# Moving one projection of a hybrid attention layer from direct products to seven-product units

## The chip, the cores and the metric

The kernel runs on one core of a Trainium2 chip. The metric is the device time of one execution in microseconds (us). Of the kernel before, three runs took 2165.18, 2166.86 and 2168.04 us; the median is 2166.86. A profile is one further execution, recorded instruction by instruction. Engines are named as the profile names them: PE is TensorE's matmul, PEld its weight load, DVE is VectorE, ACT is ScalarE, POOL is GpSimd and SP is SyncE, which only issues DMAs here. L631 is line 631 of the kernel.

## What is computed

The input x is 512 tokens by 2048 features, in float32. One layer is computed:

```
h = rmsnorm(x);  proj = h @ w_in          # 2048 x 6176
aq, ak, av (1024 columns each)            # 16 attention heads of 64
gq, gk (512 each), gv, gr (1024 each)     # 4 linear heads, key 128, value 256
glr (32)                                  # low-rank input of the forget gates
attn = softmax attention over three dilated windows, with a position bias
o    = gated linear attention, forward + backward, per-head rmsnorm, * silu(gr)
x    = x + concat(attn, o) @ w_out
x    = x + (silu(h2 @ w_gate) * (h2 @ w_up)) @ w_down,   h2 = rmsnorm(x)
out  = rmsnorm(x)
```

Queries of the linear heads are scaled by 128 to the power -1/2. All matrix products keep nearly float32 precision: each operand is split into a rounded part (hi, type fp32r) and its rest (lo), and three products are added: hi\*hi, hi\*lo, lo\*hi.

## The kernel before, in words

**Two ways to a product.** A *direct job* (`job`, `run_job`, L297 to L367) makes 512 output columns for all 512 tokens. It walks over 16 K-tiles of 128; a K-tile is called a half here, since two come in one weight piece of 512 KB. For each half it runs four *quarters*: one PSUM bank each, three matmuls of 128x128 by 128x512 (L337 to L339 in jobs of kind A, with weights stationary; L346 to L348 in kind B). The *seven-product* way (`Feed` from L1447, `Front` from L1659) is a fast scheme for 2x2 blocks: it makes 256 columns for 512 tokens from seven block products in place of eight. It needs sums of weight blocks (`sums`, L1423 to L1425 on VectorE), splits of them (L1436 on ScalarE, L1441 on VectorE) and sums of x's blocks (made once, in `xi`). A unit has four pieces of 14 products; each product is one matmul of 512 columns (L1532) and one of 256 (L1518). The end of a unit (`evac7`, from L1548) combines the seven banks on ScalarE and VectorE and adds parts by accumulating DMAs from GpSimd; `finish` multiplies by the rms factor of the tokens (`rb[1]`) and stores the result to a DRAM buffer.

**Order of the work.** Everything is emitted by one Python program in a fixed order, and every engine executes its own instructions in that order. The stages around the change are:

1. Two direct jobs for av, with the preparation of x (0 to 104 us).
2. `Front.run`: 12 seven-product units, four for gr and eight for aq and ak (104 to 339 us).
3. Four direct jobs: gq and gk of linear heads 0 and 1; gv of these; gq and gk of heads 2 and 3; gv of these (339 to 613 us). Their results are multiplied by the rms factor and stored (`evac_gqk`, L831 to L843: four VectorE operations and four DMAs; `evac_gv`: four ScalarE operations).
4. w_out on the attention half of its input: three jobs of eight halves and one of sixteen, whose second eight halves take the linear heads' outputs (613 to 742 us). Then the rest of w_out, and the feed-forward part with its own seven-product units.

**Side steps.** Attention and linear attention have no jobs. They are generators in a queue (`side`), and the jobs of stages 3 and 4 call them step by step between their quarters. Each quarter adds rate/4 to a credit; each whole credit is one call of `run_side(1)` (L350 to L353). The last quarter of a job adds none. The rate is `RATES[0]` = 2.5 in stage 3 and `RATES[1]` = 4.0 in stage 4. The queue holds the low-rank gate input (7 steps, made to last 14 calls by `slow`), then `attention` (from L713), then `silus` and the four linear heads (`gla`, two at a time by `turns`). A second queue, `urgent`, gets one step at each call as well.

**Attention's own order.** Attention has 64 units u (16 heads by 4 blocks of 128 queries) and makes two calls per unit. The first call of u emits the scores of u on TensorE (`att_scores`, L631 and L632), the scaling of u-2 for odd units (`att_scale`, L658, ScalarE), the exponential of u-1 (`att_exp`, L649, ScalarE) and the rounding of u-3 (`att_round`, L671, ScalarE), and every second time a copy (`att_lift`, L697). The second call emits the transposes of u-2 (`att_transpose`, L663), every second time the product with the values (`att_av`, L687 and L688), the rest of u-3 (`att_rest`, L677, VectorE), the bias and row maximum of u (`att_max`, L641, VectorE), every second time the mixing of two results (`att_mix`, L706, VectorE), then the reciprocal of u-1 (`att_norm`, L652) and, for even units, its scaling (L654). For each pair of heads, `load_qk` (L588, L592) splits queries and keys. A pair of heads' result becomes an operand of w_out, `mixh`: two heads of 64 features make one K-tile of 128, eight in all.

**Buffers.** SBUF slots come from two free lists (`s2`, 36 of 2 KB per partition, and `s4`, 33 of 4 KB), PSUM banks from a third of eight; the slot freed longest ago is taken first. A job holds four banks, and the side steps share the other four. The hi and lo parts of x (`hT`, 16 slots of `s4`) are given back by `free_h` when the first w_out job starts. Weights pass through `Stream` (from L180): a load from SP, then for each half a cast on ScalarE (L237) and a subtraction on VectorE (L218), some halves ahead of their use.

Of the kernel before, what the change touches and what calls it, by code (L numbers as in the profile page):

```python
# [112 lines left out]
def put(*slots):  # L113
    for s in slots:
        if s.home is not None:
            s.home.free.append(s.i)


def layer(nc, tc, x, attn_norm_w, w_in, rel_table, gw_f, gb_f, gw_b, gb_b, gla_norm_w, w_out,
# [7 lines left out]
    with tc.manual_schedule(), \  # L127
# [169 lines left out]
        def job(kind, pieces, kts, acts, evac, rate=0.0, before=None, start=None, limit=None):  # L297

            j = Job()
            j.kind, j.kts, j.acts, j.evac, j.rate, j.before, j.start, j.limit = \  # L300
                kind, kts, acts, evac, rate, before, start, limit
            j.first = len(st.halves)
            st.add(pieces)
            j.n = len(st.halves) - j.first
            jobs.append(j)
            return j
# [518 lines left out]
                G["gw"][d] = stacked(G["gw"][d], (0, 1), 2)  # L825
                yield

        gqd = dr.tile([8, P, 512], F32, name="gqd")
        gvd = dr.tile([4, P, 1024], F32, name="gvd")

        def evac_gqk(pr):  # L831
            def f(banks):
                for i in range(4):
                    t = s2.get()
                    if i < 2:
                        dve.scalar_tensor_tensor(t.t, banks[i].t, P ** -0.5, rb[1].t,
                                                 op0=OP.mult, op1=OP.mult)
                    else:
                        dve.tensor_tensor(t.t, banks[i].t, rb[1].t, op=OP.mult)
                    put(banks[i])  # L840
                    pool.dma_start(out=gqd[4 * pr + i], in_=t.t)
                    put(t)
            return f  # L843

        def load_gla(h):
            if h in gq:
                return
            for d, i in ((gq, 0), (gk, 2)):
                d[h] = s2.get()
                pool.dma_start(out=d[h].t, in_=gqd[h // 2 * 4 + i + h % 2])  # L850

        def load_gv(pr):
            gv[pr] = [s4.get(F32, [P, 2, 512]) for _ in range(2)]
# [371 lines left out]
                fr.late()  # L1225

        n_front = len(jobs)
        RATES = (2.5, 4.0)
        APART = 12
        for pr in range(2):  # L1230
            seg = [(w_in, C_GQ + pr * 256), (w_in, C_GK + pr * 256)]
            job("A", [piece512(seg, None, k) for k in range(0, KT, 2)], list(range(KT)), acts_h,
                evac_gqk(pr), rate=RATES[0], start=gstart if pr == 0 else None,
                before=None if pr else before_first, limit=3)
            job("B", [piece512(w_in, C_GV + pr * 512, k) for k in range(0, KT, 2)], list(range(KT)), acts_h,
                evac_gv(pr), rate=RATES[0],
                before=(lambda i: load_gates() if i == 12 else None) if pr else None)

        x1 = {}
        xd = dr.tile([16, P, 512], F32, name="xd")  # L1240
        gd = dr.tile([FF // 256, P, 1024], F32, name="gd")

        def free_h():
            for k in range(KT):
                put(*hT.pop(k))
            put(rb.pop(1))

        def load_res(c):
            x1[c] = []
# [97 lines left out]
        def start_out(c):  # L1347
            def f():
                if c == 1:
                    free_h()  # L1350
                if c != 1:
                    load_res(c)
            return f
# [17 lines left out]
        jobs[n_front + 3].lead = lambda i: AHEAD + (i > 11) + (i > 13)  # L1371
# [4 lines left out]
        for j in jobs[n_front + 4:]:  # L1376
# [282 lines left out]
        class Front(Feed):  # L1659


            def __init__(self):
                self.units = [(w_in, C_GR + g * 256) for g in range(4)] + \
                    [(w_in, c + g * 256) for g in range(4) for c in (C_AQ, C_AK)]
                self.per = NP // 2
                self.xs, self.wide, self.pre = xi, 0, {}
                self.begin([(u, q) for u in range(len(self.units)) for q in range(self.per)], 2, P)
# [520 lines left out]
```

## Time and profile before

| | |
|---|---|
| median of three runs | 2166.86 us (2165.18 to 2168.04) |
| the profiled execution | 2165.94 us, its span 2164.2 us |
| busy: PE, PEld, DVE, ACT, POOL | 2151.6, 1898.4, 1820.8, 1220.8, 355.0 us |
| granted TensorE clock | 0.999 |
| the chain that ended last, by engine | PE 96%, DVE 2%, DMA 1%, issue 1% |
| front, 104.4 to 339.4 us: PE, DVE, ACT busy | 234.48, 214.80, 123.27 of 235.00 us |
| attention beside direct jobs, 363.5 to 589.7 us | 225.35, 172.95, 160.08 of 226.20 us |
| w_out with linear attention, 613 to 742 us | 128.17, 102.83, 77.42 of 129.00 us |

The profile gives for each engine the time in which it executed something. Matmuls are pipelined: one of 512 columns shows a duration of about 0.39 us, while the next starts 0.23 us after it, so durations cannot be added; the distance between starts can. The page also follows the chain of work that ended last back from the end. A row of the waits names the waiting engine and line, the engine and line that ended the wait, the total, the number of waits and the longest. A row of the timeline gives start, duration, engine, line, operation with its operands (output, arrow, inputs), and in brackets the idle time of the engine before it and what ended that. The stage borders are read from the first and last instructions of the lines named above.

### The profile page before, as it was taken

To read this page: it belongs to the slowest core of one execution; us is meant where nothing else is said; L and a number is where in the kernel's file an instruction comes from. 1 tells how busy PE (TensorE), PEld (TensorE's weight loads), DVE (VectorE), ACT (ScalarE), POOL (GpSimd) and SP (SyncE) were. 2 spreads that over 40 slices of the span, in tenths; PEclk is the share of its full clock that TensorE was granted. 3 is DMA by queue.
4 is the path that set the end of the run, shared out by engine and by line. 5 is a ranking of instruction groups with operands and counts; after the bars stand their busy time and mean duration, and the time that the engine had idled before them with its cause. 6 is when DMAs were issued, how large, how long until landed. Compare 5 with 4: busy or idle time off the path is not lost.

```text
span 2164.2 us, 34918 instructions
## 1 busy us (share of the span) xinstructions
PE 2151.6 (99%) x12682; PEld 1898.4 (88%) x12682; DVE 1820.8 (84%) x3153; ACT 1220.8 (56%) x2228; POOL 355.0 (16%) x495
## 2 busy tenths in 40 slices
PE   9999999999999999999999999999999999999998
PEld 7888887888888889888888888888888899999987
DVE  6689996777768778899899899998989888888885
ACT  8455554777666446455555555555555655555562
POOL 0011213111011110012122112221122120021300
PEclk9999999999999999999999999999999999999999
DMA  6477779546475873567777667777776985576982
GB/s 203 138 178 182 178 179 256 153 129 184 128 259 175 268 243 112 145 179 182 184 178 192 174 180 188 177 186 181 180 196 172 266 211 176 177 180 159 283 307 79
DMA packets 264699, 405.71 MB, mean 187 GB/s; under 512 B 19341, under 2 KB 163389, under 8 KB 264526
## 3 DMA queue, kind: packets, MB, share of 16 engines
q1 hardware_dynamic: 206366, 274.59, 39.7%
q0 software_dynamic: 57840, 128.35, 26.5%
q8 instruction: 100, 1.64, 0.3%
q14 instruction: 73, 0.60, 0.1%
q10 hardware_dynamic: 320, 0.53, 0.1%
HBM read 287.47 MB, written 66.39 MB: 164 GB/s over the span
## 4 chain that ended last, share of the span: by engine, by line
PE 96%; DVE 2%; DMA 1%; issue 1%; ACT 0%; POOL 0%; DVEq 0%; ACTq 0%
PE ps L1532 31%; PE ps L1518 16%; PE ps L346 7%; PE ps L348 7%; PE ps L347 7%; PE ps L1891 5%; PE ps L1890 5%; PE ps L1889 5%; PE ps L339 1%; PE ps L337 1%; PE ps L338 1%; PE ps L663 1%; DMA b<-a 1%; PE ps L631 1%; PE ps L688 1%; PE ps L687 1%
## 5 line engine op out<-in xcount | busy, mean ns | idle before, releaser
L1436 ACT CAST b<-b 128x768 fp32r<-128x768 f32 (+1 forms) x569 | 519.0, 944 | 375.0 <-DVE b L1441 183.9
L1441 DVE TENSOR_TENSOR b<-b,b 128x768 fp32r<-128x768 f32 (+1 forms) x569 | 597.3, 1084 | 32.0 <-ACT b L1436 20.9
L1532 PE MATMUL ps<-b,b 128*128 128x512 f32 x1656 | 484.1, 393 | 0.4 <-ACT b L1436 0.2
L1532 PE MATMUL ps<-a,b 128*128 128x512 f32 x1368 | 401.1, 394 | 0.5 <-DVE b L1552 0.4
L1532 PEld LDWEIGHTS ps<-b,b 128*128 128x128 f32 x1656 | 280.8, 188 | 32.0 <-ACT b L1436 0.7
L1518 PEld LDWEIGHTS ps<-b,b 128*128 128x128 f32 x1656 | 271.4, 190 | 39.2
L1518 PE MATMUL ps<-b,b 128*128 128x256 f32 x1656 | 296.7, 280 | 0.0
L1518 PEld LDWEIGHTS ps<-a,b 128*128 128x128 f32 x1368 | 227.3, 189 | 36.9 <-DVE b L1441 0.6
L1532 PEld LDWEIGHTS ps<-a,b 128*128 128x128 f32 x1368 | 228.1, 189 | 23.1 <-issue 1.0
L1518 PE MATMUL ps<-a,b 128*128 128x256 f32 x1368 | 245.6, 280 | 0.2 <-DVE b L1441 0.2
L1423 DVE TENSOR_TENSOR b<-b 128x512 f32<-128x512 f32 x260 | 178.1, 685 | 16.5 <-DMA b<-in_w_down_dram 6.5
L1889 PE MATMUL ps<-b,b 128*128 128x256 f32 x624 | 176.6, 283 | 0.0
L1890 PE MATMUL ps<-b,b 128*128 128x256 f32 x624 | 176.6, 283 | 0.0
L1891 PE MATMUL ps<-b,b 128*128 128x256 f32 x624 | 176.6, 283 | 0.0
L346 PE MATMUL ps<-b,b 128*128 128x512 f32 x304 | 122.5, 403 | 0.0
L1889 PEld LDWEIGHTS ps<-b,b 128*128 128x128 f32 x624 | 119.8, 192 | 0.0
L1890 PEld LDWEIGHTS ps<-b,b 128*128 128x128 f32 x624 | 119.8, 192 | 0.0
L1891 PEld LDWEIGHTS ps<-b,b 128*128 128x128 f32 x624 | 119.8, 192 | 0.0
L348 PE MATMUL ps<-b,b 128*128 128x512 f32 x304 | 118.8, 391 | 0.0
L347 PE MATMUL ps<-b,b 128*128 128x512 f32 x304 | 118.6, 390 | 0.0
L1425 DVE TENSOR_TENSOR b<-b,b 128x256 f32<-128x256 f32 x260 | 110.6, 425 | 8.9
L1424 DVE TENSOR_TENSOR b<-b,b 128x256 f32<-128x256 f32 x260 | 110.5, 425 | 9.0
(303 smaller groups left out, 4176.9 us busy)
## 6 DMA issues: line engine op xcount, KB each, us to landing
b<-in_w_gate_dram SPq DMA_DIRECT2D x109, 512.0 KB, 3.9
b<-in_w_up_dram SPq DMA_DIRECT2D x88, 512.0 KB, 4.1
b<-in_w_down_dram SPq DMA_DIRECT2D x88, 512.0 KB, 5.5
b<-a POOLq DMA_DIRECT2D x162, 256.0 KB, 4.4
b<-in_w_in_dram SPq DMA_DIRECT2D x78, 512.0 KB, 3.8
b<-in_w_out_dram SPq DMA_DIRECT2D x32, 512.0 KB, 5.7
gd<-b POOLq DMA_DIRECT2D x22, 512.0 KB, 4.0
b<-gd SPq DMA_DIRECT2D x22, 512.0 KB, 7.8
```

Source lines behind the costliest of these rows:

```text
L346: mm(o, xh.t[:, c], wh.t[:, w], start=first and not on, stop=False, skip_group_check=on)
L347: mm(o, xh.t[:, c], wl.t[:, w], start=False, stop=False, skip_group_check=on)
L348: mm(o, xl.t[:, c], wh.t[:, w], start=False, stop=last, skip_group_check=on)
L1423: dve.tensor_tensor(s_[:, :, 0:2], r[:, :, 1:3], r[:, :, 0:1].to_broadcast(shape), op=OP.add)
L1425: dve.tensor_tensor(s_[:, :, 3], s_[:, :, 2], r[:, :, 3], op=OP.add)
L1436: act.copy(o, src)
L1441: dve.tensor_tensor(o, src, h, op=OP.subtract)
L1518: mm(o, wl, xh, start=False, stop=end, skip_group_check=True)
L1532: mm(o.rearrange("p (s t) -> p s t", s=2), wh, x_, start=first and p == 0, stop=False, skip_group_check=True)
L1889: mm(o, xh[:, t], wh, start=first and h == 0, stop=False, skip_group_check=True)
L1890: mm(o, xh[:, t], wl, start=False, stop=False, skip_group_check=True)
L1891: mm(o, xl[:, t], wh, start=False, stop=last, skip_group_check=True)
```

## The change

The projection gq, gk of linear heads 0 and 1 leaves the direct jobs. `Front` gets two more units, gq's first 256 columns and gk's first 256, after the four of gr; they are stored in a new buffer `gfd`, and `load_gla` reads heads 0 and 1 from it. In it, as in the other units' results, one of the two heads has its sign turned, for query and key alike, which cancels in the products. `finish` scales the query unit. One direct job of kind A is left (heads 2 and 3), then the two gv jobs. The rate of side steps in these jobs goes from 2.5 to 3.1, and attention's last steps now fall in the first w_out job. x's operands `hT` are given back K-tile by K-tile in the last direct job; `free_h` is gone.

```
-        gqd = dr.tile([8, P, 512], F32, name="gqd")
+        gqd = dr.tile([4, P, 512], F32, name="gqd")
+        gfd = dr.tile([2, P, 1024], F32, name="gfd")
...
         def load_gla(h):
             if h in gq:
                 return
-            for d, i in ((gq, 0), (gk, 2)):
+            for i, d in enumerate((gq, gk)):
                 d[h] = s2.get()
-                pool.dma_start(out=d[h].t, in_=gqd[h // 2 * 4 + i + h % 2])
+                pool.dma_start(out=d[h].t, in_=gfd[i][:, (1 - h) * 512:(2 - h) * 512] if h < 2 else gqd[2 * i + h % 2])
...
-        RATES = (2.5, 4.0)
+        RATES = (3.1, 4.0)
         APART = 12
+        seg = [(w_in, C_GQ + 256), (w_in, C_GK + 256)]
+        job("A", [piece512(seg, None, k) for k in range(0, KT, 2)], list(range(KT)), acts_h,
+            evac_gqk, rate=RATES[0], start=gstart, before=before_first, limit=3)
         for pr in range(2):
-            seg = [(w_in, C_GQ + pr * 256), (w_in, C_GK + pr * 256)]
-            job("A", [piece512(seg, None, k) for k in range(0, KT, 2)], list(range(KT)), acts_h,
-                evac_gqk(pr), rate=RATES[0], start=gstart if pr == 0 else None,
-                before=None if pr else before_first, limit=3)
-            job("B", [piece512(w_in, C_GV + pr * 512, k) for k in range(0, KT, 2)], list(range(KT)), acts_h,
-                evac_gv(pr), rate=RATES[0],
-                before=(lambda i: load_gates() if i == 12 else None) if pr else None)
+            j = job("B", [piece512(w_in, C_GV + pr * 512, k) for k in range(0, KT, 2)], list(range(KT)), acts_h,
+                    evac_gv(pr), rate=RATES[0],
+                    before=(lambda i: load_gates() if i == 12 else None) if pr else None)
+        j.drop = lambda k: put(*hT.pop(k))
...
-        def free_h():
-            for k in range(KT):
-                put(*hT.pop(k))
-            put(rb.pop(1))
...
                 if c == 1:
-                    free_h()
+                    put(rb.pop(1))
...
-                self.units = [(w_in, C_GR + g * 256) for g in range(4)] + \
+                self.units = [(w_in, C_GR + g * 256) for g in range(4)] + [(w_in, C_GQ), (w_in, C_GK)] + \
                     [(w_in, c + g * 256) for g in range(4) for c in (C_AQ, C_AK)]
...
-                    dve.tensor_tensor(c_.t, c_.t, rb[1].t[:, None, :].to_broadcast([P, 2, 512]), op=OP.mult)
-                    pool.dma_start(out=grd[u] if u < 4 else qkd[u - 4], in_=c)
+                    r = rb[1].t[:, None, :].to_broadcast([P, 2, 512])
+                    if u == 4:
+                        dve.scalar_tensor_tensor(c_.t, c_.t, P ** -0.5, r, op0=OP.mult, op1=OP.mult)
+                    else:
+                        dve.tensor_tensor(c_.t, c_.t, r, op=OP.mult)
+                    pool.dma_start(out=grd[u] if u < 4 else gfd[u - 4] if u < 6 else qkd[u - 6], in_=c)
```

`evac_gqk` is otherwise as before, without its parameter, and the indices by which later jobs are picked out of the list (`n_front + 3` and `n_front + 4`) are one lower.

More of the change, by code (lines that the diff above doesn't have):

```diff
@@ L826, in low_rank, with evac_gqk @@
                 yield
-        gqd = dr.tile([8, P, 512], F32, name="gqd")
+        gqd = dr.tile([4, P, 512], F32, name="gqd")
+        gfd = dr.tile([2, P, 1024], F32, name="gfd")
         gvd = dr.tile([4, P, 1024], F32, name="gvd")
[L831 to L843, printed above, removed]
+        def evac_gqk(banks):
+            for i in range(4):
+                t = s2.get()
+                if i < 2:
+                    dve.scalar_tensor_tensor(t.t, banks[i].t, P ** -0.5, rb[1].t,
+                                             op0=OP.mult, op1=OP.mult)
+                else:
+                    dve.tensor_tensor(t.t, banks[i].t, rb[1].t, op=OP.mult)
+                put(banks[i])
+                pool.dma_start(out=gqd[i], in_=t.t)
+                put(t)
         def load_gla(h):
@@ L1370, in layer @@
         n_in = len(jobs)
-        jobs[n_front + 3].lead = lambda i: AHEAD + (i > 11) + (i > 13)
+        jobs[n_front + 2].lead = lambda i: AHEAD + (i > 11) + (i > 13)
         j = job_out(0, 0, KT, evac_out(0), rate=RATES[1], start=start_out(0), before=load_first)
@@ L1375, in layer @@
         j.drop = lambda k: drop_mix(k) if k < 8 else None
-        for j in jobs[n_front + 4:]:
+        for j in jobs[n_front + 3:]:
             j.lead = lambda i: AHEAD + 4
@@ L1674, in do @@
                 def do():
-                    dve.tensor_tensor(c_.t, c_.t, rb[1].t[:, None, :].to_broadcast([P, 2, 512]), op=OP.mult)
-                    pool.dma_start(out=grd[u] if u < 4 else qkd[u - 4], in_=c)
+                    r = rb[1].t[:, None, :].to_broadcast([P, 2, 512])
+                    if u == 4:
+                        dve.scalar_tensor_tensor(c_.t, c_.t, P ** -0.5, r, op0=OP.mult, op1=OP.mult)
+                    else:
+                        dve.tensor_tensor(c_.t, c_.t, r, op=OP.mult)
+                    pool.dma_start(out=grd[u] if u < 4 else gfd[u - 4] if u < 6 else qkd[u - 6], in_=c)
                     put(c_)
```

## The prediction

> **What bounds the kernel now.** I read the page's engine rows first, then busy time by stage, then the waits of the attention stage, then the timeline inside it. In the stage table the columns are window, length, and busy time (instructions) of matmul, weight load, VectorE, ScalarE, GpSimd, then granted clock, DMA share and GB/s.
>
> ```profile
> PE 2151.6 (99%) x12682; PEld 1898.4 (88%) x12682; DVE 1820.8 (84%) x3153; ACT 1220.8 (56%) x2228; POOL 355.0 (16%) x495
> ```
>
> ```profile
> 104.40:339.40 235.00, 234.48 (x1345) 205.46 (x1344) 214.80 (x342) 123.27 (x203) 49.28 (x64) 1.00 0.74 184
> 363.50:589.70 226.20, 225.35 (x1220) 190.40 (x1220) 172.95 (x405) 160.08 (x337) 38.02 (x71) 1.00 0.50 150
> ...
> 613.00:742.00 129.00, 128.17 (x626) 107.38 (x626) 102.83 (x208) 77.42 (x181) 24.54 (x46) 1.00 0.68 229
> ```
>
> TensorE is busy nearly everywhere: the seven-product units of the front (104 to 339), attention beside the direct jobs (363 to 590), linear attention beside w_out (613 to 742). In the attention stage VectorE is busy 76% and ScalarE 71%, so by shares both have room. The waits of that stage (who waited for whom, total us, times, longest) say something else.
>
> ```profile
> DVE b L677 <- ACT b L671: 41.5, 44, 2.5
> ACT a L658 <- DVE small L652: 29.3, 24, 2.4
> ...
> ACT a L649 <- DVE small L641: 23.3, 28, 1.4
> ...
> DVE a L641 <- PE ps L632: 3.7, 5, 1.5
> ...
> PE ps L631 <- DVE b L677: 0.7, 1, 0.7
> ```
>
> VectorE and ScalarE wait for each other (94 us in these three rows) and hardly for TensorE (3.7). I followed that in the timeline, VectorE first, then ScalarE (start, duration, engine, line; the bracket is idle time before and who ended it).
>
> ```profile
> 508.45 0.69 DVE L677 TENSOR_TENSOR b<-ps,b 128x512 fp32r<-128x512 f32 x1 [0.75 <-ACT b L671]
> 509.06 0.68 DVE L641 CUSTOM_DVE_ANT_0 a<-ps,b 128x512 f32<-128x512 f32 x1
> ...
> 509.67 0.41 DVE L706 TENSOR_TENSOR a<-ps,a 64x256 f32<-64x256 f32 x1
> 510.00 0.14 DVE L652 RECIPROCAL small<-small 128x1 f32<-128x1 f32 x1
> 510.07 0.67 DVE L218 TENSOR_TENSOR a<-b,a 128x512 fp32r<-128x512 f32 x1
> 512.32 0.69 DVE L677 TENSOR_TENSOR b<-ps,b 128x512 fp32r<-128x512 f32 x1 [1.57 <-ACT b L671]
> 512.92 0.68 DVE L641 CUSTOM_DVE_ANT_0 a<-ps,b 128x512 f32<-128x512 f32 x1
> ...
> 514.97 0.69 DVE L677 TENSOR_TENSOR b<-ps,b 128x512 fp32r<-128x512 f32 x1 [0.16 <-ACT b L671]
> ```
>
> ```profile
> 508.72 0.62 ACT L237 CAST a<-b 128x512 fp32r<-128x512 f32 x1
> 510.24 0.72 ACT L658 ACTIVATE a<-a,small 128x512 f32<-128x512 f32 x1 [0.91 <-DVE small L652]
> 510.88 0.71 ACT L649 ACTIVATE a<-a,small 128x512 f32<-128x512 f32 x1
> ...
> 511.70 0.58 ACT L671 CAST b<-ps 128x512 fp32r<-128x512 f32 x1
> ...
> 513.65 0.73 ACT L649 ACTIVATE a<-a,small 128x512 f32<-128x512 f32 x1 [0.85 <-DVE small L641]
> ...
> 514.37 0.57 ACT L671 CAST b<-ps 128x512 fp32r<-128x512 f32 x1
> ```
>
> This is a closed loop. Call u one of the 64 units of attention (a head's block of 128 queries). The row maximum of u (L641) releases the exponential of u (L649); behind it on ScalarE stands the rounding of an older unit (L671), which releases its rest on VectorE (L677); behind that stands the maximum of u+1. That leg is 512.32 to 514.97, 2.65 us. Every second leg also holds L706, the reciprocal and the scaling on ScalarE (L658): 508.45 to 512.32, 3.87 us. No TensorE instruction ends a step in it. The stream's cast and subtraction (L237, L218) fall into the idle brackets.
>
> Over eight units the legs repeat; the extra work of a pair of heads (L588, L592) is in them. The next rows are maxima: a whole block (494.45 and 522.21, eight units apart), then the legs around job ends.
>
> ```profile
> 494.45 0.68 DVE L641 CUSTOM_DVE_ANT_0 a<-ps,b 128x512 f32<-128x512 f32 x1
> ...
> 522.21 0.68 DVE L641 CUSTOM_DVE_ANT_0 a<-ps,b 128x512 f32<-128x512 f32 x1
> ```
>
> ```profile
> L641 DVE CUSTOM_DVE_ANT_0 a<-ps,b x64: 679/681/692, 364.8 to 591.3; 128x512 f32<-128x512 f32 x64
> ```
>
> ```profile
> L631 PE MATMUL ps<-a,a x64: 389/395/501, 363.8 to 589.7; 128*128 128x512 f32 x64
> ```
>
> A block of eight costs the loop 27.76 us, 3.47 a unit. The scores (L631) go from 363.8 to 589.7, 225.9 us for 63 steps, 3.59 a unit. So the loop already fills 97% of the stage, and bursts at job ends take the rest: TensorE's work and the loop are in balance now, and the shares of busy time hide it.
>
> **The change part by part.**
>
> *Two more seven-product units in the front.* Steady pieces of the chain (start, us, line), one unit apart:
>
> ```profile
> 285.93 3.20 PE ps L1532 x14
> ...
> 305.43 3.20 PE ps L1532 x14
> ```
>
> A unit costs 19.5 us on TensorE, which is busy 234.48 of 235.00 there, so two cost 39.0. VectorE has 214.80 us for twelve units, 17.9 of each 19.5: it keeps up with fourteen as with twelve. The added loads, GpSimd's accumulating DMAs and stores repeat the pattern of the existing units. The query unit's closing multiply takes another form (it also scales); that is one operation, on an engine with 1.6 us a unit free. Range for all of this: 0 to +1, taken 0.
>
> *One direct job less.* It is 64 quarters (three matmuls into one bank).
>
> ```profile
> 340.08 0.39 PE L337 MATMUL ps<-b,b 128*128 128x512 f32 x1
> ...
> 340.76 0.39 PE L337 MATMUL ps<-b,b 128*128 128x512 f32 x1
> ```
>
> A quarter is 0.68 us, the job 43.5. Its sixteen casts and subtractions, SP's weight loads, four evacuations on VectorE and four stores on GpSimd go with it. TensorE's own work thus falls by 43.5 - 39.0 = 4.5 us.
>
> *Steps denser.* Side steps are released by quarters: 2.5 per four quarters before, 3.1 after (a job's last quarter gives none). The low-rank part takes 14 calls, so scores of u = 0 come with call 15 and of u = 63 with call 141. Counting credits, these calls stand 205 quarters apart before, 164 after. Inside the stage 41 quarters vanish, 27.9 us; the other 23, 15.6 us, vanish outside it, where TensorE sets the time. Inside, TensorE would need 225.9 - 27.9 = 198.0 us, 3.14 a unit. The loop does not follow, because its order of instructions is the same. What it takes: 226.5 now between the first and last maximum (364.8 to 591.3); less the burst of the evacuation that is gone:
>
> ```profile
> 547.37 0.68 DVE L641 CUSTOM_DVE_ANT_0 a<-ps,b 128x512 f32<-128x512 f32 x1
> ...
> 552.17 0.68 DVE L641 CUSTOM_DVE_ANT_0 a<-ps,b 128x512 f32<-128x512 f32 x1
> ```
>
> 4.80 against a free leg of 2.65, so 2.1; less about 2.1 of the 3.7 us in which maxima waited for scores (the first two must still wait a little); less 1.0 for the thinner stream (0.65 halves a unit instead of 0.8; where two L588 and one L218 meet in a leg, one drops out now and then). That leaves 221.3. TensorE may end ahead by more than it began: scores of u take the bank that the rest of u-4 frees (the one wait of 0.7 us above), and that rest runs just before the maximum of u-1, so scores lead their maximum by up to one leg, 3.9, say 3.5 at the end against 1.0 at the start. Scores to scores: 221.3 - 2.5 = 218.8. The stage shrinks by 225.9 - 218.8 = 7.1 us, not by 27.9: TensorE stands idle some 21 us, a third of a microsecond per unit, mostly at L631 for L677 and at the transposes (L663) for L658.
>
> This is where a rule can be weighed. By the rows TensorE has occupancy 99.6% in the stage and VectorE 76%. The Trainium skill (Perfetto Trace Analysis, Identifying the Most-Contended Engine) takes the engine of highest occupancy as the one to improve, while warning that matmul busy time is a poor measure. By that rule the time would fall with TensorE's work, to about 2162; by the loop's rows it rises. I go by the loop, since its 3.47 is measured leg by leg.
>
> *Attention ending in w_out.* The last mixed heads come in the second half of the eight of w_out's first job and are used in the eighth: six halves of 2.7 us cover that. Linear attention starts two to three halves later than before; its last output comes in half 10 (from 0) of the last of these jobs instead of half 8, used from half 14. VectorE, 80% busy from 613 to 742, then meets it beside more of the sums made ahead for the feed-forward part. Bounds 0 and +5, taken 0, since 128.17 of 129.00 is TensorE's now.
>
> *x's operands by K-tile.* No instruction is added; buffers come free earlier. TensorE waits for no buffer at the job's end now, so nothing is won; 0.
>
> Sum: +39.0 - 15.6 - 7.1 = +16.3. The profiled execution took 2165.94 us (span 2164.2), 0.9 below the median of 2166.86. So 2182.2 against the former and 2183 against the median. No change, for a measurement of this kernel, is within 0.2%, 2162.5 to 2171.2.
>
> **The rivals.**
>
> *TensorE's work decides (ends on the other side).* If ScalarE and VectorE work faster when work is denser, the stage falls to 198 and the kernel by 4.5 us, 2162: faster. For it: idle brackets on both engines, and the rule of the Trainium skill named above. Against it: each bracket is the other engine's instruction. It decides if the loop takes less than 3.14 a unit. Chance 0.12.
>
> *The stream is in the loop.* If the whole 0.62 + 0.67 us of a half (L237, L218) sat on it, 0.155 fewer halves a unit save 0.2 us, 12.6 over 63 units; 1.0 is counted already, so 2183 - 11.6 = 2171.5. Against it: in the legs shown both stand in the brackets (L218 from 510.07, while VectorE waits until 512.32). Chance 0.10, split between no change and slower.
>
> *More than the loop.* TensorE gains no lead (+2.5), and linear attention, moved on, makes w_out wait (+5): 2191; with another burst of 4 to 5 us at a job end, 2195. For it: evacuation bursts land in a loop without slack. Chance 0.08.
>
> *Loop-bound as summed.* 0.70, its own range 2176 to 2190: lead 0 to 3.5, start and stream savings 1 to 5, bursts 2 us either way.
>
> **How the numbers follow.** Slower holds the main case, the last rival and most of the stream's: 0.82. Faster is the first rival less the part in which small stalls eat its gain: 0.11. Within 0.2% is the rest, 0.07. The range must leave out no more than 0.2, so it runs from the stream case to the bad end: 2169 to 2196.
>
> **What would show it.** Right: maxima (L641) still 27 to 28 us per eight; TensorE idle some 20 us between first and last scores, with L631 and L663 waiting for VectorE or ScalarE; front 39 us longer; TensorE's busy time about 4 us less. Wrong: eight maxima in 25 to 26 us, or TensorE without gaps (first rival); legs shortened by about 0.2 a unit (second); gaps after the last scores, in w_out (third). The prediction fails if the order on VectorE or ScalarE differs from the present one, since the legs are read from it.

## The result, and the profile after

The changed kernel takes 2188.24 us, the median of five runs (2186.09 to 2190.26), against 2166.86 for the kernel before (2165.18 to 2168.04). The ratio is 1.0098, with an interval of 1.0084 to 1.0113: slower by 21.4 us. The forecast was 2183 (2169 to 2196).

The profiled execution of the changed kernel is the slowest of the five: it took 2190.26 us with a span of 2188.5 us, at a mean granted clock of 0.997 where the other four had 0.998. That of the kernel before had a span of 2164.2. So the traces differ by 24.3 us where the medians differ by 21.4, and the stages below are told in the former. Lines 631 to 706, 218, 237, 337 to 339 and 346 to 348 keep their numbers. The wide stream's lines stand 6 lower (1526 for 1532), those of linear attention 1 lower (922, 1016), and w_out's evacuation is line 1298.

The engine row of the page, after:

```profile
PE 2158.2 (99%) x12714; PEld 1897.5 (87%) x12714; DVE 1844.7 (84%) x3191; ACT 1232.7 (56%) x2246; POOL 361.2 (17%) x501
```

TensorE's busy time rose by 6.6 us although by the forecast it has 4.5 us less to do. Busy time of matmuls is no measure of their work here. Matmuls that follow each other closely overlap in the records (0.39 us each, but 0.23 apart), and that overlap goes when they are spread out by waits or by a slower clock.

Busy time by stage, after (window, length, then matmul, weight load, VectorE, ScalarE, GpSimd, each with its instructions, granted clock, DMA share, GB/s):

```profile
105.00:379.30 274.30, 273.02 (x1565) 239.29 (x1564) 251.15 (x399) 143.29 (x236) 56.95 (x74) 1.00 0.74 183
401.70:618.90 217.20, 204.97 (x1097) 166.12 (x1096) 163.65 (x388) 153.16 (x325) 36.08 (x67) 0.99 0.53 153
619.00:863.00 244.00, 238.52 (x1142) 198.94 (x1141) 189.12 (x403) 138.15 (x305) 36.94 (x69) 0.99 0.64 213
540.00:560.00 20.00, 17.63 (x92) 14.69 (x91) 11.52 (x28) 14.80 (x31) 5.28 (x10) 0.91 0.59 161
640.00:660.00 20.00, 16.57 (x74) 13.50 (x73) 14.78 (x27) 12.97 (x24) 0.55 (x1) 0.95 0.72 259
660.00:680.00 20.00, 20.00 (x90) 17.11 (x90) 15.40 (x30) 10.04 (x20) 2.08 (x4) 0.88 0.32 111
```

The difference of 24.3 us by stages, from the same marks in both traces (the starts of the first seven-product matmul, the first direct one, the first and the last scores, and the first matmul of the feed-forward part):

| stage | before | after | difference | forecast |
|---|---|---|---|---|
| seven-product units of the front | 235.2 | 275.0 | +39.8 | +39.0 |
| direct jobs up to the first scores (4 quarters fewer) | 24.4 | 22.4 | -2.0 | -2.7 |
| first to last scores (41 quarters fewer) | 225.9 | 216.8 | -9.1 | -7.1 |
| last scores to the feed-forward part (19 quarters fewer) | 249.2 | 244.5 | -4.7 | -12.9 |
| all the rest | | | +0.4 | 0 |

Two stages fail to give back what their lost quarters are worth (0.68 us each): attention gives 9.1 of 27.9, which was forecast, and the stage from the last scores on gives 4.7 of 12.9, which was not.

In the attention stage (401.7 to 618.9), who waited for whom, total us, times, longest:

```profile
DVE b L677 <- ACT b L671: 44.5, 47, 2.2
...
ACT a L658 <- DVE small L652: 29.4, 23, 3.0
ACT a L649 <- DVE small L641: 24.4, 25, 2.1
...
PEld ps L663 <- ACT a L658: 12.4, 19, 0.9
...
PEld ps L631 <- DVE b L677: 8.7, 14, 2.0
```

VectorE and ScalarE wait for each other as before, in the same three rows (98 us; before the change 94). The row of maxima that waited for scores (L641 for L632) fell from 3.7 to 2.7 us. What is new is that TensorE waits, for the rest (L677) and for the scaled weights (L658). Two maxima eight units apart, in the timeline of VectorE after, and the scores' group:

```profile
484.92 0.68 DVE L641 CUSTOM_DVE_ANT_0 a<-ps,b 128x512 f32<-128x512 f32 x1
...
512.07 0.68 DVE L641 CUSTOM_DVE_ANT_0 a<-ps,b 128x512 f32<-128x512 f32 x1
```

```profile
L631 PE MATMUL ps<-a,a x64: 389/395/628, 401.9 to 618.7; 128*128 128x512 f32 x64
```

These eight units take 27.15 us, where TensorE alone would have needed 25.1 by the forecast (8 x 3.14). It is one of the quick blocks: two maxima eight apart are 25.8 to 31.4 us apart in this trace, 27.9 in the mean over all 63 steps, and in the kernel before 26.0 to 32.4, in the mean 28.8. So this block can't be held against the 27.76 of the one shown before; the kernel before has blocks of 27.15 too (412.89 to 440.04). The scores run from 401.9 to 618.7.

Next, TensorE's waits in the whole run (the four largest, then one more at w_out), and its timeline at the end of w_out's first job with VectorE's behind it:

```profile
PE ps L663 <- ACT a L658: 4.5, 12, 0.5
PE ps L631 <- DVE b L677: 4.2, 6, 1.6
PE ps L1016 <- DVE b L1298: 3.4, 1, 3.4
PE ps L663 <- ACT b L861: 2.4, 1, 2.4
...
PE ps L922 <- DVE b L1298: 0.9, 1, 0.9
```

```profile
655.26 0.39 PE L348 MATMUL ps<-b,a 128*128 128x512 f32 x1
659.08 1.12 PE L1016 MATMUL ps<-idn,a 128*128 128x128 f32 x4 [3.43 <-DVE b L1298]
...
662.13 0.63 PE L347 MATMUL ps<-b,a 128*128 128x512 f32 x1
662.55 0.63 PE L348 MATMUL ps<-b,a 128*128 128x512 f32 x1
...
667.30 0.40 PE L347 MATMUL ps<-b,a 128*128 128x512 f32 x1
667.53 0.39 PE L348 MATMUL ps<-b,a 128*128 128x512 f32 x1
```

```profile
655.60 0.68 DVE L218 TENSOR_TENSOR b<-b,b 128x512 fp32r<-128x512 f32 x1
656.21 1.28 DVE L981 TENSOR_TENSOR a<-a,a 128x512 f32<-128x512 f32 x2
657.41 0.41 DVE L1486 TENSOR_TENSOR b<-b 128x256 f32<-128x256 f32 x1
657.75 2.47 DVE L1298 TENSOR_TENSOR b<-b,ps 128x512 f32<-128x512 f32 x4
```

The key transposes of the first linear head (L1016) now come right behind the last matmul of w_out's first job. They need a bank that this job's evacuation (L1298) frees, and VectorE does other things first (the stream's subtraction, two operations of linear attention, a sum for the feed-forward part), so TensorE stands still for 3.43 us. Then it works at half speed: matmuls of 512 columns start 0.42 us apart at 662 and 0.23 apart at 667. The stage rows show that as granted clock, 0.95 and 0.88 in two windows of 20 us. Clock records are whole or half, so 0.05 x 40 + 0.12 x 40 = 6.8 us ran at half clock. The same happens on a smaller scale behind the 2.4 us wait for L861 (an evacuation of a direct job) in 540 to 560: 0.09 x 40 = 3.6 us, one record of 3.4. The kernel before has none of it until its last microseconds.

### The profile page after: what moved, and what is told of

It reads as the page before. It is cut to its first block, busy times and chain, and to the rows that moved or that the text cites. A ratio compares the mean times of both kernels' runs of the same rounds, so it can differ in the third digit from the quotient of the medians.

```text
span 2188.5 us, 35086 instructions
## 1 busy us (share of the span) xinstructions
PE 2158.2 (99%) x12714; PEld 1897.5 (87%) x12714; DVE 1844.7 (84%) x3191; ACT 1232.7 (56%) x2246; POOL 361.2 (17%) x501
## 4 chain that ended last, share of the span: by engine, by line
PE 57%; DVE 0%; DMA 0%; issue 0%; ACT 0%; DVEq 0%; ACTq 0%
PE ps L1526 24%; PE ps L1512 12%; PE ps L1889 5%; PE ps L1888 5%; PE ps L1887 5%; PE ps L347 1%; PE ps L346 1%; PE ps L348 1%; PE ps L2084 1%; PE ps L2083 1%; PE ps L2082 1%; DMA gd<-b 0%; DVE b L1435 0%; DVE a L2115 0%; DVE a L1546 0%
## 5 line engine op out<-in xcount | busy, mean ns | idle before, releaser
L1430 ACT CAST b<-b 128x1024 fp32r<-128x1024 f32 (+1 forms) x585 | 533.8, 944 | 391.2 <-DVE b L1435 196.7
L1435 DVE TENSOR_TENSOR b<-b,b 128x1024 fp32r<-128x1024 f32 (+1 forms) x585 | 613.8, 1084 | 32.6 <-ACT b L1430 20.3
L1526 PE MATMUL ps<-b,b 128*128 128x512 f32 x1708 | 500.7, 393 | 0.4 <-ACT b L1430 0.2
L1526 PE MATMUL ps<-a,b 128*128 128x512 f32 x1428 | 418.8, 394 | 1.3 <-DVE b L1546 0.6
L1526 PEld LDWEIGHTS ps<-b,b 128*128 128x128 f32 x1708 | 289.5, 188 | 32.5 <-ACT b L1430 0.7
L1512 PEld LDWEIGHTS ps<-b,b 128*128 128x128 f32 x1708 | 280.6, 190 | 40.8
L1512 PE MATMUL ps<-b,b 128*128 128x256 f32 x1708 | 307.4, 280 | 0.0
L1512 PEld LDWEIGHTS ps<-a,b 128*128 128x128 f32 x1428 | 237.0, 189 | 38.2 <-DVE b L1435 0.7
L1526 PEld LDWEIGHTS ps<-a,b 128*128 128x128 f32 x1428 | 238.5, 188 | 25.2 <-ACT b L1430 1.8
L1512 PE MATMUL ps<-a,b 128*128 128x256 f32 x1428 | 256.6, 280 | 0.3 <-DVE b L1435 0.3
L1417 DVE TENSOR_TENSOR b<-b 128x512 f32<-128x512 f32 x268 | 183.3, 684 | 18.9 <-PE ps L1889 7.1
L1887 PE MATMUL ps<-b,b 128*128 128x256 f32 x624 | 176.6, 283 | 0.0
L1888 PE MATMUL ps<-b,b 128*128 128x256 f32 x624 | 176.6, 283 | 0.0
L1889 PE MATMUL ps<-b,b 128*128 128x256 f32 x624 | 176.6, 283 | 0.0
L346 PE MATMUL ps<-b,b 128*128 128x512 f32 x348 | 140.4, 404 | 0.0
L348 PE MATMUL ps<-b,b 128*128 128x512 f32 x348 | 136.3, 392 | 0.2 <-DVE b L459 0.2
L347 PE MATMUL ps<-b,b 128*128 128x512 f32 x348 | 136.2, 391 | 0.0
L1418 DVE TENSOR_TENSOR b<-b,b 128x256 f32<-128x256 f32 x268 | 114.0, 425 | 9.3
L1419 DVE TENSOR_TENSOR b<-b,b 128x256 f32<-128x256 f32 x268 | 113.9, 425 | 9.2
L1887 PEld LDWEIGHTS ps<-b,b 128*128 128x128 f32 x624 | 119.8, 192 | 0.0
L1888 PEld LDWEIGHTS ps<-b,b 128*128 128x128 f32 x624 | 119.8, 192 | 0.0
L1889 PEld LDWEIGHTS ps<-b,b 128*128 128x128 f32 x624 | 119.8, 192 | 0.0
```

What stands on the lines that cost most here:

```text
L346: mm(o, xh.t[:, c], wh.t[:, w], start=first and not on, stop=False, skip_group_check=on)
L347: mm(o, xh.t[:, c], wl.t[:, w], start=False, stop=False, skip_group_check=on)
L348: mm(o, xl.t[:, c], wh.t[:, w], start=False, stop=last, skip_group_check=on)
L1417: dve.tensor_tensor(s_[:, :, 0:2], r[:, :, 1:3], r[:, :, 0:1].to_broadcast(shape), op=OP.add)
L1418: dve.tensor_tensor(s_[:, :, 2], s_[:, :, 0], r[:, :, 2], op=OP.add)
L1430: act.copy(o, src)
```

## The experiments

The theory: the closed loop between VectorE and ScalarE (maximum L641, exponential L649, rounding L671 behind it on ScalarE, rest L677, next maximum) sets the pace of attention, so that fewer quarters between its steps save little. The rivals: TensorE's own work sets it; the stream (L237, L218) is in the loop; or the loss lies in w_out. None of these kernels leaves work out; two of them add copies that nothing uses. The text between an edit and its measurement is what was written ahead of the run. "Scores" below means from the first to the last scores, by their starts.

### Density alone

The kernel before with nothing but the denser steps (3.1 calls for four quarters instead of 2.5 until the second gv job, 0.7 behind it, so that w_out finds things as they were):

```diff
-                evac_gqk(pr), rate=RATES[0], start=gstart if pr == 0 else None,
+                evac_gqk(pr), rate=RATES[0] + 0.6, start=gstart if pr == 0 else None,
-                evac_gv(pr), rate=RATES[0],
+                evac_gv(pr), rate=(RATES[0] + 0.6, 0.7)[pr],
```

> The kernel before with its four direct jobs, side steps at 3.1 in the first three and 0.7 in the fourth, so that as many steps as before are made by their end: the same work, only denser. Loop theory: first to last scores stay at the loop's pace, 216 to 220 us where TensorE would need 198, eight maxima still 27.5 to 27.8 us apart; the 41 quarters (28 us) that leave this stretch run alone in the fourth job; in all +17 to +21, 2184 to 2188. Rival (TensorE's work decides): no change, 2165 to 2169, the stretch at 198 to 201.

Measured: 2185.98 us (2184.42 to 2188.56), ratio 1.0092 (1.0079 to 1.0106). The scores' group and what TensorE's queue idled for ahead of them:

```profile
L631 PE MATMUL ps<-a,a x64: 387/395/507, 362.0 to 579.1; 128*128 128x512 f32 x64
...
  DVE b L677: 13.3, 20
```

Scores take 217.1 us, the same as in the changed kernel (216.8). With all of TensorE's work of before left in place, density alone makes the kernel 19.7 us slower. The quarters pushed out of the stretch cost their full time elsewhere (41 of 0.68 us, 27.9), and the stretch gives back a third (225.9 to 217.1).

### Cutting the loop

The changed kernel, with one line moved: the rounding of unit u-3 is issued ahead of the scaling and the exponential of newer units, so that the rest (L677) no longer waits behind the exponential.

```diff
                 run(att_scores, u)
+                run(att_round, u - 3)
                 run(att_scale, u - 2)
                 run(att_exp, u - 1)
-                run(att_round, u - 3)
```

> The changed kernel with one line moved: on ScalarE the rounding of unit u-3 is emitted ahead of the scaling of u-2 and the exponential of u-1. The same instructions, but the rounding no longer stands behind the exponential that waits for the last maximum, so the loop from one maximum to the next is cut. Loop theory: first to last scores fall from 217 to 198 to 204, eight maxima 25 to 26 us apart, the kernel to 2170 to 2177 (the 6 to 8 us lost later, in w_out, stay). Rival (VectorE and ScalarE are out of capacity, or the PSUM banks' recycling holds TensorE): within 4 us of the changed kernel, 2184 to 2190.

Measured: 2171.48 us (2169.34 to 2174.5), ratio 1.0024 (1.0013 to 1.0035); 16.8 us less than the changed kernel. Its attention stage and its scores:

```profile
401.30:600.90 199.60, 197.79 (x1096) 167.03 (x1096) 165.55 (x393) 152.85 (x327) 35.78 (x67) 1.00 0.56 168
```

```profile
L631 PE MATMUL ps<-a,a x64: 389/393/497, 401.3 to 600.7; 128*128 128x512 f32 x64
...
  DVE b L677: 1.0, 2
```

199.4 us, where the prediction had worked out 198.0 as TensorE's own need; the maxima (L641, 402.4 to 601.4) are 25.3 us apart per eight in the mean. No operation was added or taken away, and VectorE and ScalarE are as busy as in the changed kernel (165.55 and 152.85 us, against 163.65 and 153.16). So it was the order on ScalarE and not the amount of work. The wait at w_out is still there (L1016 for L1298, 3.4 us, and half clock for 6.8 us behind it), and with it the time stays above that of the kernel before.

### The same cut where the loop still fits

The same line moved in the kernel before.

> The kernel before with the rounding ahead of scaling and exponential on ScalarE, as in the run that moved this line in the changed kernel. Loop theory: in the kernel before the loop (27.8 us per eight units) is still shorter than TensorE's work (28.7), so cutting it wins only the few waits at job ends, 0 to 3 us: 2163.5 to 2166.5. Rival (the new order is better in itself, whatever the density): about as much as the changed kernel won by it, 15 us.

Measured: 2165.73 us, ratio 0.9998 (0.9989 to 1.0006); scores 363.9 to 589.9, 225.9 us. With 2.5 calls for four quarters TensorE needs as long as the loop, and a faster loop wins nothing.

### More ScalarE work, in the loop and beside it

The kernel before, with two small copies on ScalarE a unit (298 ns each), once between the exponential and the rounding, once behind the lift of the attention values:

```diff
                 run(att_exp, u - 1)
+                for _ in range(2):
+                    act.copy(warm, idn)
                 run(att_round, u - 3)
```

> The kernel before with two small copies (128 columns, some 0.25 us each, an estimate from the 0.37 us of 256 columns and 0.62 us of 512) added per attention unit on ScalarE, between the exponential and the rounding. Loop theory: legs grow by 0.4 to 0.5, eight maxima take about 31 us, the kernel becomes 20 to 28 us longer, 2187 to 2195, though ScalarE's share in the stretch only rises from 71% to some 83%. Rival (TensorE's work decides, ScalarE has room): no change, 2165 to 2169.

```diff
                     run(att_lift, (u - 6) // 2, UNITS // 2)
+                for _ in range(2):
+                    act.copy(warm, idn)
                 yield
```

> The same two copies, at the end of ScalarE's work in a unit's first call, behind the rounding and the lift. Loop theory: they fall into the idle time in which ScalarE waits for the next maximum; eight maxima stay near 28 us, the kernel +0 to +4, 2166 to 2171. Rival (ScalarE's capacity decides): the same growth as with the copies between exponential and rounding.

Measured: in the loop 2187.29 us, ratio 1.0098 (1.0083 to 1.0114); beside it 2167.17 us, ratio 1.0003 (0.9994 to 1.0012). Their attention stages, first the one, then the other:

```profile
363.50:610.00 246.50, 235.79 (x1223) 187.79 (x1222) 171.32 (x402) 190.75 (x463) 37.94 (x71) 1.00 0.46 139
```

```profile
363.10:589.60 226.50, 225.11 (x1220) 190.39 (x1219) 172.94 (x405) 191.30 (x464) 38.05 (x71) 1.00 0.49 148
```

ScalarE is busy for the same time in both (190.75 and 191.30 us). In the one place 38 us of copies (64 x 0.6) cost 20; in the other they cost nothing. This pair separates the loop from ScalarE's load. In the second, ScalarE's share is 84% and nothing happens; in the first it is 77% and the stage grows by 20 us.

### The other link of the loop

The changed kernel with the maximum of u ahead of the rest of u-3 on VectorE:

```diff
-                run(att_rest, u - 3)
                 run(att_max, u)
+                run(att_rest, u - 3)
```

> The changed kernel with another cut of the same loop: on VectorE the row maximum of u is emitted ahead of the rest of u-3, and ScalarE's order is untouched. Loop theory: the maximum no longer stands behind a rest that waits for the rounding, so first to last scores fall from 217 to 198 to 206 and the kernel to 2170 to 2178, as with the rounding first. Rival (the rounding's own place on ScalarE matters, not the loop): within 4 us of the changed kernel, 2184 to 2190.

Measured: 2177.46 us, ratio 1.0052 (1.0037 to 1.0067); scores 401.4 to 606.5, 205.1 us. Cut at this link, the stretch loses 11.7 of its 216.8 us, not as much as by the other cut (17.4), and the scores now wait for maxima (L631 for L641, 3.8 us at five places). The wait at w_out and both stretches of half clock remain.

### Linear attention later, in the kernel before

The kernel before, with eleven empty steps ahead of linear attention, so that it meets the end of w_out's first job as it does after the change:

```diff
                     act.activation(g, g, AF.Silu, scale=1.0 - 2.0 * f)
                 yield
+            for _ in range(11):
+                yield
```

> The kernel before with eleven empty side steps ahead of linear attention, so that it stands against the w_out jobs where the change puts it; nothing else is touched. If the position is what costs time in w_out (transposes of the first head right behind the first w_out job's evacuation on VectorE, whose banks they take): +4 to +7, 2170 to 2173, with a wait of about 3.4 us at the first transposes of the keys. Rival (the loss in w_out comes from attention's tail running there, or from x's operands being given back earlier): no change, 2165 to 2168.

Measured: 2175.47 us (2173.92 to 2176.11), ratio 1.0042 (1.003 to 1.0055), 9.3 us more, although no instruction was added. TensorE's largest waits and the window with them (evacuation and transposes have the line numbers of this kernel):

```profile
PE ps L1019 <- DVE b L1306: 6.1, 1, 6.1
...
PE ps L925 <- DVE b L1306: 0.9, 1, 0.9
```

```profile
640.00:660.00 20.00, 15.89 (x72) 13.67 (x73) 15.84 (x30) 11.24 (x24) 0.54 (x1) 0.83 0.32 115
```

The wait is there, longer than in the changed kernel (6.1 against 3.4 us), and so is the half clock (0.17 x 40 = 6.8 us). The half clock reaches 5.2 us behind the end of the wait (644.11 to 649.32), and nearly half of that is lost. Waits of 7.0 us and these 2.4 make 9.4 against the measured 9.3. The expectation had the wait but not the clock, and so was too low.

### Attention and linear attention earlier, in the changed kernel

The changed kernel without the delay of the low-rank part, which moves everything behind it seven steps ahead:

```diff
-            side.append(slow(low_rank()))
+            side.append(low_rank())
```

> The changed kernel with the low-rank part making its seven steps in seven calls instead of fourteen, so that attention and linear attention stand seven steps earlier against the jobs: the first head's transposes come in half 6 of the first w_out job, not right behind its evacuation. The attention stretch is untouched. If the position makes the loss in w_out: the wait of 3.4 us there and the half clock of 6.8 us behind it (which costs some 3 us) go, the first to last scores stay at 216 to 219 us, the kernel is at 2181 to 2184. Rival (the half clock and the loss come from the stretch of attention before it): 2186 to 2190, the half clock still there.

Measured: 2194.01 us (2193.31 to 2194.56), ratio 1.013 (1.0113 to 1.0147). A miss, by 10 us in the wrong direction; only half of its expectation came true. From the last scores to the feed-forward part it takes 246.0 us, with nine quarters (6.1 us) more of direct work in it than the changed kernel has in its 244.5. There is no half clock there, and so some 4.6 of the 8.2 us are gone. But "the stretch untouched" was wrong: scores run from 394.5 to 621.4, 226.9 us. VectorE at the beginning, and TensorE's largest wait:

```profile
399.43 0.69 DVE L588 SCALAR_TENSOR_TENSOR a<-a,a 128x512 fp32r<-128x512 f32 x1
400.04 1.22 DVE L1673 TENSOR_TENSOR b<-b,a 128x1024 f32<-128x1024 f32 x1
401.17 0.69 DVE L1546 TENSOR_TENSOR b<-b,a 128x512 f32<-128x512 f32 x1
401.77 0.68 DVE L641 CUSTOM_DVE_ANT_0 a<-ps,b 128x512 f32<-128x512 f32 x1
```

```profile
PE ps L631 <- DVE b L677: 7.7, 7, 3.5
```

The first maximum comes 7.3 us behind its scores (394.5 to 401.77), instead of 1.1 (401.9 to 403.0), because splits of keys and queries (L588) and of the low-rank part (L794) and the front's last sums (L1673, L1546) stand ahead of it on VectorE. That late start is 6.2 of the 10.1 us by which the stretch is longer; the other 3.9 lie between first and last maximum (223.3 us instead of 219.4) and were not traced to a line. There TensorE waits for up to 3.5 us at a time, and two stretches of half clock follow (at 404.4 and 421.5, 3.4 and 6.8 us long).

### What the change is worth with the loop cut

The changed kernel with the rounding moved ahead, as above, and other densities:

```diff
-        RATES = (3.1, 4.0)
+        RATES = (3.35, 4.0)
```

> The changed kernel with the rounding first and side steps at 3.35 in place of 3.1, which puts linear attention back to where it stands in the kernel before (first head's transposes in half 5 of the first w_out job). If both found causes are the whole loss: the 6 us of w_out go, the stretch of attention takes 190 to 196 us where 194 is TensorE's need, and the kernel is at 2162 to 2167, the 4.5 us of saved TensorE work less what VectorE, then busy some 88%, makes wait. Rival (VectorE is out of capacity at this density): 2170 or more, with waits of TensorE all along the stretch.

Measured: 2164.89 us (2163.2 to 2166.62), ratio 0.9995 (0.9986 to 1.0004); scores 398.6 to 590.0, 191.4 us. No half clock is recorded, and TensorE's largest wait is 1.3 us.

The same with 3.3 calls:

> Rounding first and side steps at 3.3 in place of 3.35. Linear attention starts two to three steps later against the w_out jobs, and VectorE has a little more room in the stretch: 2163 to 2166, the same as at 3.35 within what can be told.

Measured: 2166.86 us, ratio 1.0003 (0.9995 to 1.0012). Again one wait at the first linear head (L1016, 1.3 us).

The same as the first (3.35) with three empty steps ahead of linear attention:

> Rounding first, side steps at 3.35, and three empty side steps ahead of linear attention, so that its first matmul no longer stands right behind the evacuation of the last direct job, where the run without these steps waited 1.3 us for a bank. If that wait is simply the position: about 1.5 us less than there, 2162 to 2164.5. Rival (another border is met instead, as linear attention has one at every w_out job): 2165 to 2169.

Measured: 2163.9 us (2163.36 to 2168.55), ratio 0.9991 (0.9982 to 1.0). The lowest median of all, 2.7 us under the kernel before measured beside it (2166.56), with an interval that reaches 1. By itself it isn't told from the kernel before, nor from the one above.

And at 3.35 calls with both links cut:

> Rounding first on ScalarE and maximum ahead of the rest on VectorE, side steps at 3.35. If after the first cut no loop holds TensorE any more, the second wins nothing or up to 1.5 us: 2163 to 2166. If a rest of the loop through the values' rest still costs at 3.35: up to 3 us less, 2162.

Measured: 2170.26 us (2167.15 to 2172.07), ratio 1.0013 (1.0004 to 1.0023); scores 399.5 to 595.4, 195.9 us. A miss: the second cut adds 4.5 us to the stretch, where it was to add nothing. TensorE waits for scaled weights there (L663 for L658, 1.9 us at four places). The trace shows no half clock; its execution took 2168.79 us at a granted clock of 0.999, and the seven slowest of the eleven (2169.57 and up) had 0.997 or 0.998, so half clock adds to the median. Why the two cuts don't go together stays open.

## Why the prediction was right, and where it wasn't

**The loop: right, as a mechanism and nearly in size.** Attention was to shrink by 7.1 us and not by 27.9; it shrank by 9.1. Maxima are 27.9 us apart per eight in the mean, 27.15 in the block shown (27 to 28 forecast). The lead of the scores over their maxima grew from 1.1 us at the first unit to 3.7 at the last (618.7 to 622.4), where 3.5 was forecast. First to last maximum took 219.4 us (403.0 to 622.4), where 221.3 was. Inside that sum the terms didn't come as set down: maxima wait 1.0 us less for scores (3.7 to 2.7), where 2.1 was taken off, so that the evacuation that is gone and the thinner stream together gave 6.1 and not 3.1 us; how the 6.1 divide was not traced. That 221.3 lies so near is in part luck. TensorE waits at L631 and at the transposes, as foretold. "Some 20 us idle" holds by the starts (216.8 against the 198.0 of TensorE's own need); the profile records 12.2 us without a matmul (204.97 busy of 217.20), since spread-out matmuls overlap less. The rivals on this point fell: had TensorE decided, scores would have taken 198; had the stream been in the loop as the second rival has it, density alone would have cost some 8 us (11.6 less) and not 19.7. The experiments show the cause and do not only agree with it: the line moved on ScalarE gives 16.8 us back, and the copies cost 20 us in the loop and none beside it.

By the rule that was weighed, of the Trainium skill (Perfetto Trace Analysis, Identifying the Most-Contended Engine), the engine of highest occupancy is to be optimised first, and TensorE's headroom is judged by MFU or the busy share of its weight loads. By weight loads too TensorE stood highest in the attention stage before: 190.40 of 226.20 us, 84%, against VectorE's 76%. The change relieved it by 4.5 us of work, and the time rose by 21.4; here the measurement decides against taking the highest share for the bound. The warning of the Trainium skill in the same section, that matmul busy time is not a good measure of how close TensorE is to its roofline, fits the trace: it rose by 6.6 us while the work fell.

**The front: right.** +39.8 against +39.0; the range for what isn't in the 39.0 was 0 to +1. From trace to trace this stage varies by as much (234.0 to 235.6 us in the six kernels without the change, 273.1 to 275.0 in the eight with it).

**Attention ending in w_out: wrong in size; this is the term that failed.** It was bounded by 0 and +5 and taken as 0, "since 128.17 of 129.00 is TensorE's now". It measured +8.2: 12.9 us were to vanish behind the last scores, and 4.7 did. The wait at L1016 is 3.4 of it, the one at L922 0.9. The half clock costs some 2.7: of its 6.8 us 5.8 lie behind the wait (659.08 to 664.89), and at 0.42 us a matmul instead of 0.23 nearly half of that is lost. The remaining 1.2 us was not traced to a line. The reasoning had VectorE and its load in view, but not the order: linear attention, some steps later, asks for a bank just when w_out's first evacuation has to free it. The third rival named that ("linear attention, moved on, makes w_out wait") at +5. The experiments show it to be the position: with linear attention alone moved onto that place the kernel before loses 9.3 us, and moved off it, together with attention, the changed kernel loses some 4.6 us less there. The clock was in no part of the prediction.

**Smaller points.** Quarters ahead of the first scores saved 2.0 of 2.7 us. TensorE's busy time was to fall by about 4 us and rose by 6.6; this was a mistake in the sign to look for, since the busy time of spread-out matmuls grows. Gaps should have been looked for in the waits or in the starts.

**The sum.** +16.3 was forecast and +24.3 came, in the profiled executions. Of the 8.0 between them w_out is +8.2, the front +0.8, the first quarters +0.7, the attention stage -2.0, the rest +0.4. By medians it is 2183 against 2188.24, inside the likeliest case's own range (2176 to 2190); that it is so near owes something to the attention stage, which came out 2.0 us short and so hid a part of what w_out cost.

## What to carry to other kernels

Two engines that wait for each other in order can set the pace while each is busy only three quarters of the time. Take two equal instructions a whole period apart in the timeline, add up the legs between them, and compare that with what the busiest engine needs for the period before making its work denser; take several such periods, since here they ran from 25.8 to 31.4 us. Ahead of spending work to break such a loop, look whether the order of issue on one of its engines can be changed: here one moved line was worth 16.8 us. And where a stage is moved, look not only at whether its engines have room but at which border it lands on: a request for a bank right behind a job's last matmul waits until that job's evacuation gets its turn and frees one (3.4 and 6.1 us here).

## What the runs showed of the hardware

The clock drop behind a single wait was not expected. Every stretch of half clock inside these kernels stands behind waits of TensorE: 3.4 us of it behind the 2.4 us wait at 541.9 in the changed kernel and behind one of 2.4 us with density alone, 6.8 us behind 3.4 us in the changed kernel and in the one with the rounding moved, 6.8 us behind 6.1 us in the kernel before with late linear attention, 3.4 us behind 1.9 us with the maximum first. Where the largest wait was 1.3 us (with 3.35 calls) or 1.7 (there with both links cut) there was none. The lengths are 3.4 us and twice that, and the ratio was always a half.

The records say more than that. Each clock record that a kernel's start or end doesn't cut off is a multiple of 3.413 us long (in the changed kernel 158, 1, 32, 2 and 445 of them), so their borders lie on a fixed grid. Some windows of that grid in the changed kernel (columns as above; the first number behind the length is TensorE's busy time, the third from the end the clock):

```profile
542.01:545.42 3.41, 1.19 (x9) 1.03 (x10) 1.86 (x5) 3.41 (x7) 0.96 (x2) 1.00 0.12 49
545.42:548.84 3.42, 3.42 (x13) 2.84 (x12) 0.97 (x2) 2.02 (x5) 3.42 (x8) 0.50 0.99 294
654.65:658.06 3.41, 1.00 (x5) 0.50 (x3) 3.41 (x7) 2.66 (x6) 0.00 (x0) 1.00 0.37 137
658.06:661.48 3.42, 2.40 (x11) 2.41 (x12) 3.42 (x7) 0.59 (x1) 0.03 (x1) 0.50 0.00 0
661.48:664.89 3.41, 3.41 (x11) 2.72 (x11) 1.31 (x3) 0.00 (x0) 0.51 (x1) 0.50 0.38 154
419.13:422.54 3.41, 1.85 (x11) 1.24 (x10) 3.35 (x5) 1.26 (x3) 1.99 (x4) 1.00 0.59 226
```

Counted in this way over all fourteen traces, each of the 23 windows at full clock that one at half clock follows leaves TensorE at least 1.91 us without a matmul, and none of the 8828 others leaves more than 1.56. Behind a window at half clock the clock stayed at half where that window had 1.02 to 1.63 us without a matmul (five times), and was full again where it had at most 0.03 (nine times). So what went with the drop is the idle time within one window and not the length of one wait: with attention earlier, waits of 1.4 and 0.8 us fell into one (2.13 us idle, 400.99 to 404.40), and the 1.7 us wait with both links cut was divided by a border (1.37 us at most on one side).

The Trainium skill (TensorE: Matmul & The Clock Gate, Part 1: The HAM clock gate) says that the clock is either full or half, and half by default and after at least one idle window of about 3.4 us. The trace agrees on the ratio and on the unit of length. On the idle time it shows less: 1.91 us of idle time in a window of 3.41 were enough. What it costs is the wait and then somewhat less than half of the stretch behind it: 3.4 us became some 6 at w_out (3.4 and 2.7).

A second thing not expected, in the kernel and not in the chip, is how much the beginning of attention matters. With scores 7.4 us earlier, and the first maximum only 1.2, the stage took 226.9 us instead of 216.8. The loop did not make the late start up.
